# One tile per direction for the decay rows of a state-space mixer, summed and multiplied in place

## The chip, the cores and the metric

The kernel runs on one core of a Trainium2 chip. Its time is device microseconds (us) of one execution. A core has five engines with a queue of instructions each, worked off in order: TensorE (PE in the profile; PEld are its weight loads), VectorE (DVE), ScalarE (ACT), GpSimd (POOL) and SyncE (SP), which here issues most of the DMAs. They work on SBUF, a memory of 128 partitions; PE writes into PSUM. An engine that needs another's result waits at that instruction, and all behind it in its queue waits too.

## The reference, cut to what matters

The whole program is two layers of an encoder over 512 tokens with 1024 features: a mixer, a SwiGLU channel mixer and a gated embedding in each, then a norm. The change is in the first mixer, a Mamba-2 scan that runs over 8 groups of 4 heads, forwards and backwards. Within a chunk of 128 tokens one direction computes:

```python
acum = jnp.cumsum(dtc * a_gk, axis=1)
decay = jnp.exp(jnp.where(mask, acum[:, :, None] - acum[:, None], -jnp.inf))
cb = jnp.einsum('blgn,bsgn->blsg', cc, bc)
scores = cb[..., None] * decay * dtc[:, None]
y = jnp.einsum('blsgk,bsgkp->blgkp', scores, xc)
y = y + jnp.einsum('blgn,bgkpn->blgkp', cc, state) * jnp.exp(acum)[..., None]
```

So each head has a 128 by 128 matrix of decays per chunk and direction, masked to one triangle. `cb` belongs to the group and is the same for both directions but for the side of the mask. The kernel therefore adds the two decay matrices of a head first and multiplies the sum once by `cb`.

## The kernel before, in words

Features lie on the partitions and tokens along them, and the whole input stays in SBUF. Every fp32 product of a projection is made of three matmuls on a high and a low part of each factor (L292 to L294 and L677 to L679). The weights come in blocks of eight 128 by 128 tiles, 512 KB each: SP loads a block (L270), ACT casts the high part (L274), and DVE, or POOL for every other block of this mixer, subtracts it for the low part (L275). There are three buffers each for a raw block and its two parts, and a block is asked for two blocks before PE needs it.

The Python order of the program is the order in which work is given to a scheduler (the Tile framework's), which sets each engine's own order from dependences and its own estimate of when things are ready, and which gives out the buffers of the tiles. A tile waits for a buffer of its kind (its tag) until the readers of the buffer's last tile are done.

The mixer's loop runs over the groups g. In iteration g stand, in this order: the decay matrices of the group before (`mix_exp(g-1)`); the projections of group g with their convolution of five taps (`mix_in`, L591 on ACT, L595 on DVE, then the gate function at L597 and L598); the parts that come from the carried states (`mix_off`, L782 to L787); the projection of the output gate z (`mix_z`, L677 to L682); the diagonal products of the group before on its decay matrices (`mix_diag(g-1)`, L773 on PE, L775 on DVE, which adds the result into y); transposes and the matrix CB of group g (`mix_pre_a`, L688 to L707); at every odd g from 3 on the transposes of finished output (`finish`, L813 on PE into a PSUM buffer of the kind aux, of which there are four, then a cast at L323 on ACT and a subtraction at L324 on DVE); the output gate of the group before (`mix_gate`, L793 to L798: y times z, a tanh on ACT, the product, four sums of squares into `junk`); the first projections of the next group; and the chunk states (`mix_pre_b`, L723, copied out of PSUM into ST by ACT at L732 and L734 and carried on by POOL at L728 and DVE at L729, and y begun by POOL at L744).

`mix_exp` works on one head at a time. SP loads a tile FB of the head's two rows of 512 numbers, one per direction, repeated on every partition, 512 KB in all (L753). POOL sets the masked half of each direction to a value whose exponential is zero (L755, one instruction per direction), ACT takes the exponential per chunk with another bias each (L759, eight per head), DVE adds the two directions into a tile M (L761) and multiplies it by CB (L762). M stays until the diagonal products (L773). FB has 4 buffers of 4 KB per partition, M 4 of 2 KB. The same tags also serve the temporaries of the step sizes at the mixer's start (`dtt`, from L608) and, for FB, the split inputs `pp` of the gated embedding (L537); the second layer's embedding calls the same helper with its own tags (L912).

Of the kernel before, what the change touches and what calls it, by code (L numbers as in the profile page):

```python
# [10 lines left out]
F32 = mybir.dt.float32  # L11
F32R = mybir.dt.float32r
AF = mybir.ActivationFunctionType
ALU = mybir.AluOpType

P = 128
T = 512
# [6 lines left out]
NC = 4  # L24
# [191 lines left out]
def body(ctx, tc, d, out_):  # L216
    nc = tc.nc
# [314 lines left out]
    def ple_in(pool, i, tags):  # L532
        pr = {}
        for k in range(2):
            raw = pool.tile([P, T], F32, tag=tags[0], name="ppr", bufs=tags[3])
            (nc.scalar if i else nc.sync).dma_start(raw, d["pT"][i, k])
            pp = pool.tile([P, 2, T], F32R, tag=tags[1][k], name="pp", bufs=tags[2])  # L537
            pr[k] = split(raw, pp[:, 0], pp[:, 1])
        return pr
# [10 lines left out]
    def ssd(next_norm):  # L550
        pool = sctx.enter_context(tc.tile_pool(name="ssd", bufs=1))
        tags = ("pre", ("FB", "FB"), 4, 2)
# [55 lines left out]
        u = pool.tile([P, NC, 64], F32, tag="M", name="dtt", bufs=4)  # L608
        V.tensor_add(u, ps[:, 0:256].rearrange("p (c x) -> p c x", c=NC), pc("dtb", 0, 64).unsqueeze(1).broadcast_to([P, NC, 64]))

        na = pool.tile([P, NC, 64], F32, tag="M", name="dtt", bufs=4)
        V.scalar_tensor_tensor(na, u, -1.0, u, ALU.mult, ALU.min)
        e = pool.tile([P, NC, 64], F32, tag="M", name="dtt", bufs=4)
# [7 lines left out]
        q = pool.tile([P, NC, 64], F32, tag="M", name="dtt", bufs=4)  # L621
# [125 lines left out]
        def mix_exp(g, t):  # L747

            M = t["M"] = []
            for j in range(4):  # L750
                hd = 4 * g + j
                FB = pool.tile([P, 2, T], F32, tag="FB", name="FB", bufs=4)
                nc.sync.dma_start(FB, FRd[:, hd].partition_broadcast(P))  # L753
                for dr in range(2):
                    G.affine_select(FB[:, dr], FB[:, dr], pattern=[[0, NC], [1 - 2 * dr, P]], compare_op=ALU.is_ge,  # L755
                                    fill=BIG, base=0, channel_multiplier=2 * dr - 1)
                    for c in range(NC):
                        e = FB[:, dr, c * P:c * P + P]
                        A.activation(e, e, AF.Exp, bias=bcol[:, c, dr * 32 + hd:dr * 32 + hd + 1])  # L759
                m = pool.tile([P, T], F32, tag="M", name="M", bufs=4)  # L760
                V.tensor_add(m, FB[:, 0], FB[:, 1])  # L761
                V.tensor_mul(m, m, t["CB"].rearrange("p c x -> p (c x)"))  # L762
                M.append(m)
# [135 lines left out]
    def ple(i, nm, next_norm, prep):  # L899
        with tc.tile_pool(name=f"ple{i}", bufs=2) as pool:  # L900
# [11 lines left out]
            tags = ("pr", ("pp", "pp"), 2, 2)  # L912
# [245 lines left out]
```

## Time and profile before

| | |
|---|---|
| median of three runs | 1590.43 us |
| lowest and highest run | 1588.3 and 1595.03 us |
| the profiled execution, its whole time | 1591.31 us |
| the profiled execution, its span | 1589.5 us |
| PE busy | 1556.0 us, 98% of the span |
| DVE busy | 1064.6 us, 67% |
| ACT busy | 671.7 us, 42% |
| POOL busy | 195.0 us, 12% |

The span goes from the first to the last instruction of the profiled execution. The rest of its time lies around the span. The profile counts an engine as busy while an instruction of it runs, and lists the idle time in front of an instruction with what ended it. PE has a clock that the chip grants in stretches; the profile gives its mean as a part of the full 2.4 GHz, and 0.50 means 1.2 GHz. Most of PE's time is outside the first mixer, which runs from about 30 to 434 us. The engines take turns at setting PE's end there, so the stage is read by who waits for whom and not by the busy shares.

### The profile page before, as it was taken

Reading aid. Unit: us, or ns where it says so; the run is one execution under the profiler, and the core shown is the slowest. Engines: PE = TensorE matmul, PEld = TensorE weight load, DVE = VectorE, ACT = ScalarE, POOL = GpSimd, SP = SyncE. Lnnn points to the kernel's source line nnn. Section 1 sums busy time; section 2 is a strip of 40 time slices with the busy share of each in tenths; the row PEclk is TensorE's granted clock in tenths of the full one; section 3 lists DMA queues with packets and bytes.
Section 4 is the critical chain, followed back from the end, with each engine's and each line's share of the span. In section 5 each row is a group of like instructions: output and inputs, shape, how many; then the busy total and the mean of one; then the engine's idle time right before and its main releaser. Section 6 shows DMA issues by size and latency. Waiting matters only on the chain.

```text
span 1589.5 us, 19858 instructions
## 1 busy us (share of the span) xinstructions
PE 1556.0 (98%) x7698; PEld 1300.1 (82%) x7698; DVE 1064.6 (67%) x1463; ACT 671.7 (42%) x1111; POOL 195.0 (12%) x153
## 2 busy tenths in 40 slices
PE   7999999999999999999999999999999999999998
PEld 5888878888788788888888878788788888888887
DVE  6698997979845775564445678999864434434564
ACT  6486665647434322232233454343253223222355
POOL 1353444432100000000000002121000000000000
PEclk9999999999999999999999999999999999999999
DMA  7443343433233243243333344332223233233332
GB/s 244 121 145 110 119 132 106 115 104 100 86 116 113 85 138 122 94 153 103 96 93 98 110 159 144 106 107 93 67 90 96 93 95 105 93 95 103 113 101 79
DMA packets 56006, 176.53 MB, mean 111 GB/s; under 512 B 5959, under 2 KB 7175, under 8 KB 54760
## 3 DMA queue, kind: packets, MB, share of 16 engines
q1 hardware_dynamic: 46864, 151.17, 30.2%
q10 hardware_dynamic: 9048, 24.10, 4.3%
q8 instruction: 60, 0.98, 0.3%
q14 instruction: 34, 0.28, 0.1%
HBM read 164.63 MB, written 10.62 MB: 110 GB/s over the span
## 4 chain that ended last, share of the span: by engine, by line
PE 80%; DVE 10%; issue 3%; DMA 3%; ACT 2%; POOL 1%; ACTq 0%; POOLq 0%; DVEq 0%
PE mm_ps L292 23%; PE mm_ps L294 23%; PE mm_ps L293 23%; DMA FB<-FRd 2%; PE aux_ps L773 1%; PE mm_ps L678 1%; PE mm_ps L679 1%; PE mm_ps L677 1%; DVE pre L595 1%; PE aux_ps L782 1%; PE aux_ps L294 1%; PE aux_ps L293 1%; PE aux_ps L292 1%; DMA pjd<-ppo 1%; DVE w_lo L275 1%
## 5 line engine op out<-in xcount | busy, mean ns | idle before, releaser
L292 PE MATMUL mm_ps<-act,w_hi 128*128 128x512 f32 (+1 forms) x1856 | 724.9, 391 | 1.5 <-DVE hv L1022 1.0
L294 PE MATMUL mm_ps<-act,w_lo 128*128 128x512 f32 (+1 forms) x1856 | 717.2, 387 | 3.6 <-DVE w_lo L275 3.1
L293 PE MATMUL mm_ps<-act,w_hi 128*128 128x512 f32 (+1 forms) x1856 | 716.9, 386 | 0.9 <-DVE act L321 0.9
L274 ACT CAST w_hi<-w_raw 128x1024 fp32r<-128x1024 f32 x248 | 260.1, 1050 | 612.8 <-PE mm_ps L293 443.3
L292 PEld LDWEIGHTS mm_ps<-act,w_hi 128*128 128x128 f32 x1856 | 349.2, 188 | 77.7 <-issue 4.3
L294 PEld LDWEIGHTS mm_ps<-act,w_lo 128*128 128x128 f32 x1856 | 349.0, 188 | 75.7 <-DVE w_lo L275 4.0
L293 PEld LDWEIGHTS mm_ps<-act,w_hi 128*128 128x128 f32 x1856 | 349.1, 188 | 74.9 <-issue 3.6
L275 DVE TENSOR_TENSOR w_lo<-w_raw,w_hi 128x1024 fp32r<-128x1024 f32 x213 | 263.6, 1239 | 92.9 <-ACT w_hi L274 92.7
L275 POOL TENSOR_TENSOR w_lo<-w_raw,w_hi 128x1024 fp32r<-128x1024 f32 x35 | 86.4, 2468 | 781.0 <-ACT w_hi L274 781.0
L884 DVE TENSOR_TENSOR fb<-mm_ps,R 128x512 f32<-128x512 f32 x44 | 30.4, 691 | 128.8 <-PE mm_ps L294 128.8
L595 DVE SCALAR_TENSOR_TENSOR pre<-mm_ps,par,pre 128x511 f32<-128x511 f32 (+1 forms) x128 | 93.9, 741 | 6.7 <-ACT pre L591 5.9
L759 ACT ACTIVATE FB<-FB,bcol 128x128 f32<-128x128 f32 x256 | 79.8, 395 | 23.3 <-POOL FB L755 23.2
L881 DVE TENSOR_TENSOR fa<-mm_ps,R 128x512 f32<-128x512 f32 x44 | 30.3, 689 | 82.4 <-PE mm_ps L294 82.4
L892 DVE TENSOR_TENSOR h<-h,mm_ps 128x512 f32<-128x512 f32 x48 | 32.9, 686 | 72.4 <-PE mm_ps L294 72.4
L677 PE MATMUL mm_ps<-w_hi,act 128*128 128x256 f32 x256 | 73.7, 288 | 0.0
L678 PE MATMUL mm_ps<-w_lo,act 128*128 128x256 f32 x256 | 72.9, 285 | 0.5 <-DVE w_lo L275 0.5
L679 PE MATMUL mm_ps<-w_hi,act 128*128 128x256 f32 x256 | 72.4, 283 | 0.0
L755 POOL TENSOR_SCALAR_AFFINE_SELECT FB<-FB 128x512 f32<-128x512 f32 x64 | 53.3, 855 | 32.0 <-DMA FB<-FRd 23.7
L678 PEld LDWEIGHTS mm_ps<-w_lo,act 128*128 128x128 f32 x256 | 49.1, 192 | 1.0 <-DVE w_lo L275 0.7
L677 PEld LDWEIGHTS mm_ps<-w_hi,act 128*128 128x128 f32 x256 | 49.1, 192 | 0.2
L679 PEld LDWEIGHTS mm_ps<-w_hi,act 128*128 128x128 f32 x256 | 49.1, 192 | 0.0
L320 ACT CAST act<-fb 128x512 fp32r<-128x512 f32 x44 | 27.3, 622 | 32.0 <-DVE fb L885 32.0
(264 smaller groups left out, 1614.0 us busy)
## 6 DMA issues: line engine op xcount, KB each, us to landing
w_raw<-W SPq DMA_DIRECT2D x248, 512.0 KB, 3.5
FB<-FRd SPq DMA_DIRECT2D x32, 512.0 KB, 6.1
pjd<-ppo ACTq DMA_DIRECT2D x16, 256.0 KB, 2.7
Hd<-Ht ACTq DMA_DIRECT2D x4, 1024.0 KB, 4.1
Ht<-Hd ACTq DMA_DIRECT2D x4, 1024.0 KB, 4.8
pj<-pjd ACTq DMA_DIRECT2D x12, 256.0 KB, 3.6
h<-xT SPq DMA_DIRECT2D x8, 256.0 KB, 5.5
dec<-dec ACTq DMA_DIRECT2D x4, 512.0 KB, 3.8
```

What stands on the lines that cost most here:

```text
L274: A.copy(hi, raw)
L275: (G if pool_lo(b) else V).tensor_sub(lo, raw, hi.bitcast(F32))
L292: PE.matmul(ps, whi, xhi, start=start, stop=False)
L293: PE.matmul(ps, whi, xlo, start=False, stop=False)
L294: PE.matmul(ps, wlo, xhi, start=False, stop=stop)
L595: V.scalar_tensor_tensor(pre[:, a:b], ps[:, a + o:b + o], pc("cw", 5 * c + j), pre[:, a:b], ALU.mult, ALU.add)
L677: PE.matmul(o, xhi[:, cs], whi, start=k == 0 and c % 2 == 0, stop=False)
L678: PE.matmul(o, xhi[:, cs], wlo, start=False, stop=False)
L679: PE.matmul(o, xlo[:, cs], whi, start=False, stop=k == KD - 1 and c % 2 == 1)
L755: G.affine_select(FB[:, dr], FB[:, dr], pattern=[[0, NC], [1 - 2 * dr, P]], compare_op=ALU.is_ge, fill=BIG, base=0, channel_multiplier=2 * ...
L759: A.activation(e, e, AF.Exp, bias=bcol[:, c, dr * 32 + hd:dr * 32 + hd + 1])
L892: V.tensor_add(h[m], h[m], ps)
```

## The change

The tile FB of two directions becomes two tiles of one direction, 2 KB per partition each. Each is loaded by a DMA of its own (256 KB, still on SP) and goes through its select and its four exponentials alone. The sum of the two goes into the forward tile instead of into M, and the product with CB too; that tile is what the diagonal products read. M is gone. FB and M together took 4 x 4 + 4 x 2 = 24 KB per partition; the new FB has 12 buffers of 2 KB, 24 KB again. The temporaries `dtt` and the split inputs `pp` move to the new tag, `pp` as two tiles instead of one of twice the size; in the second layer two buffers of double size become four. The instructions on PE, DVE, ACT and POOL keep their number and shapes.

```diff
@@ ple_in
-            pp = pool.tile([P, 2, T], F32R, tag=tags[1][k], name="pp", bufs=tags[2])
-            pr[k] = split(raw, pp[:, 0], pp[:, 1])
+            pp = [pool.tile([P, T], F32R, tag=tags[1], name="pp", bufs=tags[2]) for _ in range(2)]
+            pr[k] = split(raw, *pp)
@@ ssd
-        tags = ("pre", ("FB", "FB"), 4, 2)
+        tags = ("pre", "FB", 12, 2)
...
-        u = pool.tile([P, NC, 64], F32, tag="M", name="dtt", bufs=4)
+        u = pool.tile([P, NC, 64], F32, tag="FB", name="dtt", bufs=12)
...
@@ mix_exp
-                FB = pool.tile([P, 2, T], F32, tag="FB", name="FB", bufs=4)
-                nc.sync.dma_start(FB, FRd[:, hd].partition_broadcast(P))
+                FB = []
                 for dr in range(2):
-                    G.affine_select(FB[:, dr], FB[:, dr], pattern=[[0, NC], [1 - 2 * dr, P]], compare_op=ALU.is_ge,
+                    f = pool.tile([P, T], F32, tag="FB", name="FB", bufs=12)
+                    nc.sync.dma_start(f, FRd[dr, hd:hd + 1].partition_broadcast(P))
+                    G.affine_select(f, f, pattern=[[0, NC], [1 - 2 * dr, P]], compare_op=ALU.is_ge,
                                     fill=BIG, base=0, channel_multiplier=2 * dr - 1)
                     for c in range(NC):
-                        e = FB[:, dr, c * P:c * P + P]
+                        e = f[:, c * P:c * P + P]
                         A.activation(e, e, AF.Exp, bias=bcol[:, c, dr * 32 + hd:dr * 32 + hd + 1])
-                m = pool.tile([P, T], F32, tag="M", name="M", bufs=4)
-                V.tensor_add(m, FB[:, 0], FB[:, 1])
+                    FB.append(f)
+                m = FB[0]
+                V.tensor_add(m, m, FB[1])
                 V.tensor_mul(m, m, t["CB"].rearrange("p c x -> p (c x)"))
@@ ple of the second layer
-            tags = ("pr", ("pp", "pp"), 2, 2)
+            tags = ("pr", "pp", 4, 2)
```

The scheduler puts the instructions of all engines but PE in another order in this mixer. PE's rows stay as they are up to the last group, and behind the mixer every engine's order is the same. The lines of `mix_exp` count on in the changed kernel: the load is L755, the select L756, the exponential L760, the sum L763 and the product L764, and what stood at L775 and behind stands two lines further down.

On ACT, at iteration 3, right behind the diagonal of the third group, from the copy of CB on (L323 is `finish`, L794 the tanh, L798 the squares, L591 the convolution's first step, L274 a weight cast), before:

```order
L702 COPY CB<-aux_ps 128x512
L323 ACTIVATE act<-aux_ps,par 128x512
L794 ACTIVATE z<-z 128x1024
L323 ACTIVATE act<-aux_ps,par 128x512
L759 ACTIVATE FB<-FB,bcol 128x128 x8
L798 ACTIVATE junk,ssq<-y 128x256 x4
L591 ACTIVATE pre<-mm_ps,par 128x512
L732 COPY ST<-aux_ps 128x256
L734 COPY ST<-aux_ps 128x256
L274 CAST w_hi<-w_raw 128x1024
```

and in the changed kernel, where the squares are L800 and the exponentials L760:

```order
L702 COPY CB<-aux_ps 128x512
L323 ACTIVATE act<-aux_ps,par 128x512
L760 ACTIVATE FB<-FB,bcol 128x128 x3
L323 ACTIVATE act<-aux_ps,par 128x512
L800 ACTIVATE junk,ssq<-y 128x256 x4
L760 ACTIVATE FB<-FB,bcol 128x128 x5
L274 CAST w_hi<-w_raw 128x1024
L591 ACTIVATE pre<-mm_ps,par 128x512
L732 COPY ST<-aux_ps 128x256
L734 COPY ST<-aux_ps 128x256
```

Eight exponentials stand between the casts of `finish` and the copies of ST in both; the squares now stand ahead of five of them, the tanh has moved further ahead, and a weight cast now stands in front of the copies.

On DVE, in the same place, from the weight subtraction ahead of the diagonal's results on (L775 takes these out of PSUM, L793 and L795 are the output gate, L707 weights the chunk inputs, L761 is the sum and L762 the product with CB), before:

```order
L275 TENSOR_TENSOR w_lo<-w_raw,w_hi 128x1024
L775 TENSOR_TENSOR y<-y,aux_ps 128x512
L761 TENSOR_TENSOR M<-FB 128x512
L775 TENSOR_TENSOR y<-y,aux_ps 128x512
L761 TENSOR_TENSOR M<-FB 128x512
L793 TENSOR_TENSOR y<-y,z 128x1024
L707 TENSOR_TENSOR xw<-XT,wS 128x3x256 x2
L324 SCALAR_TENSOR_TENSOR act<-aux_ps,par,act 128x512 x2
L795 SCALAR_TENSOR_TENSOR y<-z,y 128x1024
L762 TENSOR_TENSOR M<-M,CB 128x512 x2
L761 TENSOR_TENSOR M<-FB 128x512 x2
L762 TENSOR_TENSOR M<-M,CB 128x512
```

and in the changed kernel:

```order
L275 TENSOR_TENSOR w_lo<-w_raw,w_hi 128x1024
L777 TENSOR_TENSOR y<-y,aux_ps 128x512 x2
L795 TENSOR_TENSOR y<-y,z 128x1024
L707 TENSOR_TENSOR xw<-XT,wS 128x3x256 x2
L797 SCALAR_TENSOR_TENSOR y<-z,y 128x1024
L324 SCALAR_TENSOR_TENSOR act<-aux_ps,par,act 128x512 x2
L764 TENSOR_TENSOR FB<-FB,CB 128x512 x4
L763 TENSOR_TENSOR FB<-FB 128x512
L275 TENSOR_TENSOR w_lo<-w_raw,w_hi 128x1024
L595 SCALAR_TENSOR_TENSOR pre<-mm_ps,par,pre 128x510
```

The sums (L761 before) between the diagonal's results are gone from this place. The four products with CB stand in a row, and one sum (L763) stands ahead of a weight subtraction.

On POOL, in the first group (L744 begins y, L728 carries the states), before:

```order
L744 TENSOR_TENSOR y<-XT,par 128x1024
L275 TENSOR_TENSOR w_lo<-w_raw,w_hi 128x1024
L755 AFFINE_SELECT FB<-FB 128x512 x4
L728 TENSOR_TENSOR stt<-ST,eL 128x256 x2
L755 AFFINE_SELECT FB<-FB 128x512 x2
```

and in the changed kernel:

```order
L744 TENSOR_TENSOR y<-XT,par 128x1024
L756 AFFINE_SELECT FB<-FB 128x512 x2
L275 TENSOR_TENSOR w_lo<-w_raw,w_hi 128x1024
L756 AFFINE_SELECT FB<-FB 128x512 x4
L728 TENSOR_TENSOR stt<-ST,eL 128x256 x2
```

The two selects of the first head have moved ahead of a weight subtraction.

## Rows read from the trace of the kernel before

**Rows 1.** The page's first section: engine, busy us (share of span), instructions.

```profile
PE 1556.0 (98%) x7698; PEld 1300.1 (82%) x7698; DVE 1064.6 (67%) x1463; ACT 671.7 (42%) x1111; POOL 195.0 (12%) x153
```

**Rows 2.** Windows: us, PE PEld DVE ACT POOL busy (count), PEclk, DMA share, GB/s.

```profile
30.00:434.00 404.00, 394.72 (x2275) 336.63 (x2275) 349.95 (x499) 248.88 (x552) 148.75 (x126) 0.99 0.37 111
218.80:222.10 3.30, 3.19 (x12) 2.90 (x13) 3.16 (x8) 3.30 (x10) 1.76 (x3) 0.50 0.77 200
314.40:317.70 3.30, 3.30 (x10) 2.52 (x9) 3.30 (x7) 3.00 (x10) 1.36 (x3) 0.50 0.99 219
1101.90:1105.20 3.30, 3.26 (x28) 3.29 (x29) 3.30 (x5) 0.59 (x1) 0.00 (x0) 1.00 0.38 103
```

**Rows 3.** Timeline of PE: start, us, engine, line, operation, tiles, [idle before <-releaser].

```profile
92.79 0.50 PE L294 MATMUL mm_ps<-act,w_lo 128*128 128x512 f32 x1 [1.46 <-DVE w_lo L275]
...
218.91 0.90 PE L813 MATMUL aux_ps<-ident,y 128*128 128x128 f32 x3 [3.55 <-ACT ST L732]
...
313.31 0.44 PE L813 MATMUL aux_ps<-ident,y 128*128 128x128 f32 x2 [2.13 <-ACT ST L732]
...
1101.94 0.63 PE L1053 MATMUL aux_ps<-ident,act 128*128 128x128 f32 x4 [1.84 <-DVE act L1034]
```

**Rows 4.** Waits, 60 to 440 us: who <- for whom: us in total, times, longest.

```profile
POOL FB L755 <- DMA FB<-FRd: 23.7, 15, 5.8
ACT FB L759 <- POOL FB L755: 23.2, 12, 5.0
```

**Rows 5.** Waits of PE, 30 to 440 us.

```profile
PE aux_ps L813 <- ACT ST L732: 5.7, 2, 3.5
...
PE aux_ps L813 <- DVE act L324: 0.6, 1, 0.6
PE mm_ps L678 <- DVE w_lo L275: 0.5, 1, 0.5
```

**Rows 6.** Timeline of ACT, 204 to 220 us.

```profile
209.53 0.67 ACT L323 ACTIVATE act<-aux_ps,par 128x512 fp32r<-128x512 f32 x1
213.50 1.28 ACT L759 ACTIVATE FB<-FB,bcol 128x128 f32<-128x128 f32 x4 [3.30 <-POOL FB L755]
...
216.25 0.40 ACT L798 ACTIVATE junk<-y 128x256 f32<-128x256 f32 x1
...
218.51 0.35 ACT L732 COPY ST<-aux_ps 128x256 f32<-128x256 f32 x1
```

**Rows 7.** Chain of work that ended last, 0 to 480 us: start, us, what.

```profile
204.64 8.07 DMA FB<-FRd
...
300.45 6.35 DMA FB<-FRd
```

**Rows 8.** Tile FB, 0 to 440 us: count, ns min/median/max, first and last start.

```profile
L753 SPq DMA_DIRECT2D FB<-FRd x32: 359/377/1366, 68.8 to 362.2; - x32
L761 DVE TENSOR_TENSOR M<-FB x32: 676/690/2659, 85.2 to 407.3; 128x512 f32<-128x512 f32 x32
...
DMA to landing us min/median/max: 4.9/6.1/11.1
```

**Rows 9.** Waits of SP's DMA queue, 0 to 480 us.

```profile
SPq L270 <- DVE w_lo L275: 199.6, 39, 22.0
```

**Rows 10.** The page's DMA issues: count, KB each, median us to landing.

```profile
pjd<-ppo ACTq DMA_DIRECT2D x16, 256.0 KB, 2.7
```

**Rows 11.** Timelines of POOL and of ACT in the first group.

```profile
74.70 3.06 POOL L275 TENSOR_TENSOR w_lo<-w_raw,w_hi 128x1024 fp32r<-128x1024 f32 x1
...
89.49 1.04 ACT L274 CAST w_hi<-w_raw 128x1024 fp32r<-128x1024 f32 x1
```

**Rows 12.** Timelines of POOL and of DVE from 204 us.

```profile
204.14 2.70 POOL L275 TENSOR_TENSOR w_lo<-w_raw,w_hi 128x1024 fp32r<-128x1024 f32 x1 [6.57 <-ACT w_hi L274]
...
205.12 2.27 DVE L761 TENSOR_TENSOR M<-FB 128x512 f32<-128x512 f32 x1
...
213.21 1.33 DVE L795 SCALAR_TENSOR_TENSOR y<-z,y 128x1024 f32<-128x1024 f32 x1
```

More of the change, by code (lines that the diff above doesn't have):

```diff
@@ L606, in sm @@
             return pool.tile([P, NC, 64], F32, tag=name, name=name)
-        u = pool.tile([P, NC, 64], F32, tag="M", name="dtt", bufs=4)
+        u = pool.tile([P, NC, 64], F32, tag="FB", name="dtt", bufs=12)
         V.tensor_add(u, ps[:, 0:256].rearrange("p (c x) -> p c x", c=NC), pc("dtb", 0, 64).unsqueeze(1).broadcast_to([P, NC, 64]))
-        na = pool.tile([P, NC, 64], F32, tag="M", name="dtt", bufs=4)
+        na = pool.tile([P, NC, 64], F32, tag="FB", name="dtt", bufs=12)
         V.scalar_tensor_tensor(na, u, -1.0, u, ALU.mult, ALU.min)
-        e = pool.tile([P, NC, 64], F32, tag="M", name="dtt", bufs=4)
+        e = pool.tile([P, NC, 64], F32, tag="FB", name="dtt", bufs=12)
         elast = A.activation(e, na, AF.Exp)
@@ L620, in ssd @@
         V.tensor_mul(s2, s, s)
-        q = pool.tile([P, NC, 64], F32, tag="M", name="dtt", bufs=4)
+        q = pool.tile([P, NC, 64], F32, tag="FB", name="dtt", bufs=12)
         V.tensor_scalar_mul(q, s2, 1.0 / 19.0)
```

## The prediction

> **What bounds the kernel now.** I read the page's head first: TensorE (PE) is busy for 1556.0 us of a span of 1589.5 [rows 1], so only 33.5 us of the whole run are PE idle time, and a change that leaves PE's instructions alone can win no more than its share of them. The change touches the first mixer. The view by windows gives that stage, 30 to 434 us: PE 394.72 of 404.00 busy, so 9.28 us of idle time [rows 2]. The timeline of PE shows where most of it lies: 1.46 us before 92.79, 3.55 before 218.91, 2.13 before 313.31 [rows 3]; the other 2.1 us are six gaps of under 0.6. After the two long ones the granted clock is 0.50, that is 1.2 instead of 2.4 GHz, over windows of 3.3 us [rows 2]; half rate over 3.3 us loses 1.65 us each time, and this stands in the busy time, not in the idle time. So all that this stage can give back is 9.3 + 3.3 = 12.6 us, 0.8% of the run.
>
> Next, who causes the waits. In the list of waits GpSimd (POOL) waits 23.7 us for the FB loads and ScalarE (ACT) 23.2 us for POOL's selects on FB [rows 4], and PE 5.7 us, in two waits, for ACT's ST copies (L732) [rows 5]. The timeline of ACT around the longest one shows how these hang together: the cast at 209.53 is done at 210.20, then ACT stands 3.30 us before the exponentials at 213.50 [rows 6], since the FB load issued at 204.64 took 8.07 us [rows 7]; behind the exponentials queue the squares, the conv's first step and the ST copies at 218.51 [rows 6], and these free the PSUM buffer that PE's transposes (L813) want at 218.91. At 313.31 it is the same chain with a load of 6.35 us [rows 7]. Why is that load so late? It needs an FB buffer, which only the add into M frees, and the add needs an M buffer, which only the preceding group's diagonal products free. So every burst of loads starts just behind a diagonal, where ACT and DVE have most to do.
>
> **The change part by part.** *Buffers.* FB's 4 x 4 KB and M's 4 x 2 KB per partition become 12 x 2 KB: the same 24 KB. The add is in place, so it waits for no M; it frees the backward half at once, and the forward half stays as the masked matrix until its group's diagonal. Before, a group's adds all stand behind the diagonal of the group just ahead; in the new order, from the fourth group on, three of four stand ahead even of the diagonal before that one. This is the gain: work moves out of the burst.
>
> *Arithmetic.* The same 256 exponentials, 64 selects, 32 adds and 32 products, on the same shapes. PE's order is the same row by row up to the last group. Cost of this part: nothing on any engine.
>
> *Loads.* 32 loads of 512 KB become 64 of 256 KB: 32 more issues of 0.38 us [rows 8], 12.2 us on SP over 350 us. SP waits 199.6 us of the first 480 for weight subtractions alone [rows 9], which hides it; without that cover each issue would delay the weight load behind it by 0.38 us. What a half takes to land no row shows. Bounds: 2.7 us, another 256 KB transfer that overlaps little [rows 10], and 8.07, the load that hurt [rows 7]; the fastest whole load took 4.9 [rows 8]. I take 4.7: half the bytes, but a weight load or a second half beside it. The Trainium skill speaks against small loads (DMA: Bandwidth & Descriptors, Bandwidth: batch to 1 MiB or more; Anatomy of one DMA: about 2.0 us fixed plus bytes over 436 GB/s). By its figures a whole load would be an estimated 3.2 us and each half 2.6; the trace's 4.9 is above that, so the trace decides, and with the page's 2.6 the sum below would gain 1 us more.
>
> *First group.* POOL starts the weight subtraction at 74.70 and it lasts 3.06 us [rows 11]; in the new order two selects of the first head stand ahead of it, not behind. The first load was issued at 68.84 and a whole one takes at least 4.9 [rows 8], so its halves are there by 74.7: ACT's first exponentials start near 75.4 instead of 78.4. Then the subtraction comes in between, and the other three heads start near 79.6: 24 exponentials of 0.31 (four in 1.28 us [rows 6]) and a tanh of 0.6 end near 87.7, where ACT's weight cast stands at 89.49 now [rows 11]. DVE's subtraction of that block comes 1.7 us earlier with it, and PE's 1.46 us there [rows 3], with 0.28 just before, shrink to about 0.2. Gain 1.5 us; between 0 (the first half late) and 1.74.
>
> *The wait at 218.91.* PE could go on at 218.91 - 3.55 = 215.4. The loads that ACT meets here will wait for PE's diagonal alone and no longer for a DVE add behind it: the first goes out near 203.9 instead of 204.64. With 4.7 us it lands at 208.6; POOL, free from 206.84 [rows 12], selects until 209.2; three exponentials and the second cast (0.67) end near 211. The squares also need y from DVE, done at 214.5 now [rows 12]: two adds ahead of it are gone, but the y*z product now meets POOL's subtraction that ends at 206.84, the one that stretched an add to 2.27 us [rows 12]. I put y at 211.5. Then squares and conv step 2.2 us (216.3 to 218.5 now [rows 6]), five exponentials 1.6, one weight cast of 1.0 that the new order puts ahead of the copies, and a copy of 0.35: 216.7. PE waits 1.4 instead of 3.55: gain 2.1. At 2.7 us per half the wait would be 0.9; at 8.07 the chain ends near 219.5, and PE waits 4.1, 0.6 longer than now. *The wait at 313.31* by the same steps: PE ready at 311.2, copy done near 312.6, wait 1.4 instead of 2.13, gain 0.7; between a gain of 1.2 and a loss of 0.6. *The clock.* The two drops followed idle times of 3.55 and 2.13 us; 1.84 us before 1101.94 was followed by full clock, 1.00 [rows 2, 3]. Waits of 1.4 us should leave it: gain 2 x 1.65 = 3.3, or 0.
>
> *Small gaps.* Waits of 0.5 and 0.6 us lie behind DVE work that the burst crowds [rows 5], and near the last group's end no add is left. Of the 2.1 us I take 0.7.
>
> *Against it.* The adds now stand amid the conv steps; DVE takes its queue in order, so an exponential that is late holds the conv steps, the PSUM evictions and the weight subtractions behind the add, and PE after them. And the last half of each group is released only by a diagonal. I book 1 us for it, with ends at 0 and 12 (below).
>
> Sum: 1.5 + 2.1 + 0.7 + 3.3 + 0.7 - 1.0 = 7.3 us less. The profiled execution took 1591.3 us, of which 1589.5 are the span; the median of the runs is 1590.43, 0.9 lower. I set the sum against the median: 1583.1, and say **1583 us**.
>
> **The rivals.** *All waits go* (chance 0.15): the halves land in under 4 us and ACT never meets one that is missing; 1590.4 - 12.6 = 1577.8. For it: most of the exponentials leave the burst. Against: ACT has as many instructions as now between the diagonal and the copies, plus one cast.
>
> *The wait stays* (0.25): the change does not do what it says, since the last half of a group still needs a diagonal, as M did, and lands 8 us later, behind a weight load and beside three other halves. Then the first group's 1.5 us and perhaps 0.5 of small gaps are won, and 0.6 is lost twice: 1590.4 - 0.8 = 1589.6. For it: the 8.07 stood beside weight loads, and the new order has them too.
>
> *Slower* (0.10): the add of a group's last head stands directly ahead of a weight subtraction on DVE. It is ready at landing + 0.64 + four exponentials, the last of them behind the squares; DVE gets there about 13 us after the diagonal. If landing passes 8 us, towards the 11.1 of the slowest load here [rows 8], DVE idles up to 3 us at each of six groups. DVE is idle for 404.00 - 349.95 = 54 us of the stage [rows 2], so part of it is caught up; I count 2 us each as reaching PE: 12 less 1.5 of the first group, 1601. A second thing pulls the same way: the 64 selects spread over stretches in which DVE adds and multiplies, and an add, 0.69 in the median, took 2.27 beside a POOL operation [rows 8, 12]. The Trainium skill (SBUF — State Buffer, SBUF: two separate sides) calls the port pair of the two engines an exclusive lock, held for a whole instruction; the trace agrees, as that add ended 0.55 after POOL's 206.84. By the rule a meeting costs up to one POOL instruction, and a select of 0.64 is too short to decide alone.
>
> **How the numbers follow.** Forecast 0.50 (own range 1580 to 1586), all waits go 0.15, the wait stays 0.25, slower 0.10. A measurement of this kernel can tell about 0.5%, 8 us, from no change: faster means below 1582.5. That takes the 0.15 and about half of the forecast's 0.50: 0.39. The other half and the rival that keeps the wait give 0.51 for the same, and 0.10 is slower. The range leaves out the slower case and the very ends: 1578 to 1591.
>
> **What would show it.** Right: PE's gap at the first group under 0.5 us; the two long gaps under 1.9 us with granted clock 1.00 behind them; ACT's wait before the exponentials that follow the cast of the odd groups under 1 us; POOL's wait for FB well under 23.7 us; FB landing in the median between 3.5 and 5 us. Wrong: an FB landing of 6 us or more in spite of half the size, a PE wait for ACT's ST copies of over 3 us, or DVE idle time before the adds (L763) that PE repeats a few us later.

## The result, and the profile after

The changed kernel took **1600.86 us** (median of four runs, 1600.54 to 1601.71) against 1589.37 for the kernel before on the same chip: a ratio of 1.007, with a 95% interval of 1.0056 to 1.0084. Forecast were 1583 us with a range of 1578 to 1591. The change makes the kernel slower by 0.7%, and the time is outside the range. It is the number of the rival named "slower" (1601), but by luck: that rival needed halves that land after 8 us or more, and the slowest half that the profile shows took 5.5. The losses that the experiments show lie elsewhere.

The page's head after, to be read beside [rows 1]:

```profile
PE 1562.9 (98%) x7698; PEld 1304.8 (82%) x7698; DVE 1068.1 (67%) x1463; ACT 670.5 (42%) x1111; POOL 210.0 (13%) x153
```

The span is 1599.2 us, 9.7 longer (the medians of the runs lie 11.5 apart). PE does the same 7698 matmuls, yet it is busy 6.9 us longer: the clock, as the windows below show. Only 2.8 us more are idle time. POOL has the same 153 instructions and is busy 15 us longer, so some of them last longer.

The timeline of PE after, at the waits that matter (start, us, engine, line, operation, tiles, count, idle before with its releaser), beside [rows 3]:

```profile
94.63 0.51 PE L294 MATMUL mm_ps<-act,w_lo 128*128 128x512 f32 x1 [3.62 <-DVE w_lo L275]
172.97 0.48 PE L723 MATMUL aux_ps<-xw,BT 128*128 128x256 f32 x1 [1.63 <-DVE xw L707]
175.63 0.77 PE L723 MATMUL aux_ps<-xw,BT 128*128 128x256 f32 x1 [1.96 <-DVE xw L707]
227.46 0.66 PE L815 MATMUL aux_ps<-ident,y 128*128 128x128 f32 x4 [1.72 <-ACT ST L732]
310.99 0.69 PE L695 MATMUL aux_ps<-ident,sx 128*128 128x128 f32 x2 [2.56 <-DVE y L777]
323.39 0.66 PE L815 MATMUL aux_ps<-ident,y 128*128 128x128 f32 x4 [0.55 <-ACT ST L732]
...
439.16 0.39 PE L294 MATMUL mm_ps<-act,w_lo 128*128 128x512 f32 x1
```

The fourth and the sixth of these are the two long waits of [rows 3], for the ST copies: 3.55 became 1.72, and 2.13 became 0.55. This is what the change was forecast to do. The first is the first group's wait, which was to vanish and grew to 3.62. The others are new. The last row stands just behind the mixer, and before the same matmul stood here:

```profile
431.69 0.39 PE L294 MATMUL mm_ps<-act,w_lo 128*128 128x512 f32 x1
```

So the mixer ends 7.5 us later. The other 2.2 us of the 9.7 come behind it, where all orders are the same; 1.5 of them arise at a stretch of half clock near 1136 us, which a second trace of the changed kernel does not have (`after_again`, below).

Busy time by windows after (us, then PE, PEld, DVE, ACT and POOL busy with counts, granted clock, DMA share, GB/s):

```profile
95.50:98.80 3.30, 3.30 (x9) 2.60 (x8) 3.30 (x5) 0.39 (x2) 2.69 (x2) 0.50 0.78 191
174.00:180.70 6.70, 5.07 (x8) 2.77 (x9) 6.70 (x7) 4.38 (x16) 5.62 (x5) 0.50 0.34 134
224.00:228.00 4.00, 2.28 (x10) 0.97 (x9) 4.00 (x6) 4.00 (x12) 2.68 (x4) 1.00 0.00 0
310.50:313.80 3.30, 2.81 (x13) 2.81 (x14) 3.27 (x3) 2.05 (x4) 2.37 (x1) 0.50 0.74 209
323.00:327.00 4.00, 3.61 (x20) 3.17 (x21) 4.00 (x7) 3.53 (x12) 2.45 (x2) 1.00 0.36 87
1010.30:1013.50 3.20, 3.20 (x9) 2.49 (x8) 3.20 (x7) 2.98 (x5) 0.00 (x0) 0.50 0.98 347
```

The clock stays at full rate behind the two waits for ST, as forecast. But at each of the three places where waits grew or are new there is a stretch at 1.2 GHz, and three more that the kernel before does not have lie outside the mixer: near 1010 (the last row), 17 and 1136 us. At half rate a stretch loses half of its busy time: 1.65, 2.5 and 1.4 us in the mixer.

From the starts of PE the 7.5 us of the mixer add up roughly: 3.5 in the first group (94.63 less 92.79, and the clock behind it), 7 near 173 (waits of 0.9 shortly before, 1.63 and 1.96, and the clock), 4 near 311, less 3.5 and 3.2 at the two waits for ST (1.8 and 1.6 of idle time, 1.65 of clock each) and some 0.5 of small gaps.

### The profile page after: what moved, and what is told of

It reads as the page before. It is cut to its first block, busy times and chain, and to the rows that moved or that the text cites. A ratio compares the mean times of both kernels' runs of the same rounds, so it can differ in the third digit from the quotient of the medians.

```text
span 1599.2 us, 19907 instructions
## 1 busy us (share of the span) xinstructions
PE 1562.9 (98%) x7698; PEld 1304.8 (82%) x7698; DVE 1068.1 (67%) x1463; ACT 670.5 (42%) x1111; POOL 210.0 (13%) x153
## 4 chain that ended last, share of the span: by engine, by line
PE 80%; DVE 10%; issue 4%; ACT 3%; DMA 2%; POOL 1%; SPq 0%; ACTq 0%; POOLq 0%; DVEq 0%
PE mm_ps L292 23%; PE mm_ps L294 23%; PE mm_ps L293 23%; DMA FB<-FRd 1%; PE aux_ps L775 1%; DVE xw L707 1%; PE mm_ps L678 1%; PE mm_ps L677 1%; PE mm_ps L679 1%; PE aux_ps L294 1%; PE aux_ps L293 1%; PE aux_ps L292 1%; PE aux_ps L784 1%; DVE w_lo L275 1%; DVE act L321 1%
## 5 line engine op out<-in xcount | busy, mean ns | idle before, releaser
L274 ACT CAST w_hi<-w_raw 128x1024 fp32r<-128x1024 f32 x248 | 260.1, 1050 | 610.8 <-PE mm_ps L293 445.1
L275 POOL TENSOR_TENSOR w_lo<-w_raw,w_hi 128x1024 fp32r<-128x1024 f32 x35 | 93.7, 2676 | 739.2 <-ACT w_hi L274 739.2
L760 ACT ACTIVATE FB<-FB,bcol 128x128 f32<-128x128 f32 x256 | 81.0, 392 | 58.6 <-POOL FB L756 58.6
L756 POOL TENSOR_SCALAR_AFFINE_SELECT FB<-FB 128x512 f32<-128x512 f32 x64 | 58.3, 929 | 71.1 <-DMA FB<-FRd 53.9
```

What stands on the lines that cost most here:

```text
L274: A.copy(hi, raw)
L275: (G if pool_lo(b) else V).tensor_sub(lo, raw, hi.bitcast(F32))
L756: G.affine_select(f, f, pattern=[[0, NC], [1 - 2 * dr, P]], compare_op=ALU.is_ge, fill=BIG, base=0, channel_multiplier=2 * dr - 1)
```

## Three chains behind the new waits

**Near 173 us.** The timelines of DVE, SP, POOL, ACT, DVE again and POOL again, in this order, follow one half tile of FB:

```profile
160.85 0.69 DVE L763 TENSOR_TENSOR FB<-FB 128x512 f32<-128x512 f32 x1 [0.26 <-ACT FB L760]
...
161.57 0.32 SPq L755 DMA_DIRECT2D FB<-FRd  x1
...
164.91 1.50 POOL L756 TENSOR_SCALAR_AFFINE_SELECT FB<-FB 128x512 f32<-128x512 f32 x1 [5.47 <-DMA FB<-FRd]
...
166.45 1.28 ACT L760 ACTIVATE FB<-FB,bcol 128x128 f32<-128x128 f32 x4 [4.24 <-POOL FB L756]
167.64 1.06 ACT L682 ACTIVATE z<-mm_ps 128x512 f32<-128x512 f32 x2
...
170.01 1.09 ACT L696 COPY XT<-aux_ps 128x512 f32<-128x512 f32 x2
...
171.12 4.36 DVE L707 TENSOR_TENSOR xw<-XT,wS 128x768 f32<-128x768 f32 x2 [5.21 <-ACT XT L696]
...
169.72 2.39 POOL L275 TENSOR_TENSOR w_lo<-w_raw,w_hi 128x1024 fp32r<-128x1024 f32 x1 [3.30 <-ACT w_hi L274]
172.06 2.61 POOL L744 TENSOR_TENSOR y<-XT,par 128x1024 f32<-128x1024 f32 x1
```

A sum ends at 161.5 and frees a half tile; the load goes out at 161.57 and lands 3.2 us later; POOL, which waited 5.47 us, masks it; ACT, which waited 4.24 us, takes its four exponentials at 166.45; only then come the copies of z and XT, which were ready before, then xw on DVE, and PE had to wait. The load at 161.57 is the 31st of 64: it belongs to the fourth group's last head. The group whose XT is being copied here is the third, and the fourth group's diagonal is two diagonals away. So ACT stood still for work that nobody needed for some 90 us.

The late load is not all of it. The two xw take 4.36 us together, while POOL subtracts weights and begins y beside them (the last two rows). In the kernel before no work of POOL ran beside them, and they took:

```profile
164.68 1.81 DVE L707 TENSOR_TENSOR xw<-XT,wS 128x768 f32<-128x768 f32 x2
```

PE's second wait here, 1.96 us before 175.63, is for the second xw. That POOL slows them is argued from the first group (below), not shown by a run of its own. A slow xw alone does not make PE wait: without the late load (`a_noload35`, below) the two take 3.95 us, start at 165.94, and PE has no wait at L723.

**Near 311 us** it is the same, one step longer (timelines of DVE, SP, POOL, ACT, DVE). The load is the 55th, of the seventh group:

```profile
300.93 0.68 DVE L763 TENSOR_TENSOR FB<-FB 128x512 f32<-128x512 f32 x1
...
301.63 0.32 SPq L755 DMA_DIRECT2D FB<-FRd  x1
...
305.68 0.64 POOL L756 TENSOR_SCALAR_AFFINE_SELECT FB<-FB 128x512 f32<-128x512 f32 x1 [5.95 <-DMA FB<-FRd]
...
306.35 1.28 ACT L760 ACTIVATE FB<-FB,bcol 128x128 f32<-128x128 f32 x4 [4.28 <-POOL FB L756]
...
310.26 1.28 DVE L777 TENSOR_TENSOR y<-y,aux_ps 128x512 f32<-128x512 f32 x2
```

Behind the exponentials wait the convolution's gate, a weight cast, and with them on DVE the last gate product, a weight subtraction and the reading of the diagonal out of PSUM; PE's next transposes (L695) need that PSUM buffer.

**In the first group** it is another thing. The timelines of DVE and POOL after:

```profile
85.44 1.80 DVE L763 TENSOR_TENSOR FB<-FB 128x512 f32<-128x512 f32 x2
87.16 1.11 DVE L764 TENSOR_TENSOR FB<-FB,CB 128x512 f32<-128x512 f32 x1
...
93.36 1.22 DVE L275 TENSOR_TENSOR w_lo<-w_raw,w_hi 128x1024 fp32r<-128x1024 f32 x1
...
85.00 3.76 POOL L756 TENSOR_SCALAR_AFFINE_SELECT FB<-FB 128x512 f32<-128x512 f32 x4
```

and the same two places before:

```profile
85.16 0.68 DVE L761 TENSOR_TENSOR M<-FB 128x512 f32<-128x512 f32 x1
...
91.08 1.65 DVE L275 TENSOR_TENSOR w_lo<-w_raw,w_hi 128x1024 fp32r<-128x1024 f32 x1
...
90.61 1.04 POOL L755 TENSOR_SCALAR_AFFINE_SELECT FB<-FB 128x512 f32<-128x512 f32 x1 [5.82 <-DMA FB<-FRd]
```

The sums and products start at the same time, but the weight subtraction behind them, for which PE waits, starts 2.3 us later. Before, POOL's next selects began at 90.61, when DVE was nearly done. Now the second group's halves are there early, POOL masks four of them from 85.00 on, and both engines take longer: a product 1.11 us, a select 0.94.

How far the exponentials run ahead is seen in the view of the tile FB, cut off at about 200 us, shortly before the third group's diagonal: it counts those that had started by then (line, engine, operation, count: duration in ns min/median/max, first and last start). The kernel before:

```profile
L759 ACT ACTIVATE FB<-FB,bcol x128: 385/393/414, 78.4 to 191.2; 128x128 f32<-128x128 f32 x128
```

The changed kernel:

```profile
L760 ACT ACTIVATE FB<-FB,bcol x152: 384/389/413, 76.3 to 200.2; 128x128 f32<-128x128 f32 x152
```

The changed kernel with the edge of `a_holdCB` (below):

```profile
L760 ACT ACTIVATE FB<-FB,bcol x96: 386/397/410, 76.2 to 180.8; 128x128 f32<-128x128 f32 x96
```

The kernel before with the edges of `b_mix` (below):

```profile
L761 ACT ACTIVATE FB<-FB,bcol x96: 384/391/409, 79.2 to 175.9; 128x128 f32<-128x128 f32 x96
```

A group has 32. Only three groups, 96, are needed by then. The kernel before was one group ahead; the changed one is nearly two.

## The experiments

All times are medians beside runs of the kernel before on the same chip (1588.4 to 1589.8 us); the ratio is to these. The theories: **A**, the order, in which exponentials stand ahead of urgent work on ACT and wait there for loads; **B**, collisions of POOL and DVE; **C**, the 64 small loads by themselves.

**Exponentials held behind their own group's CB copy** (`a_holdCB`). Tiles and loads are those of the changed kernel; an edge in the scheduler puts the exponentials behind an instruction on ACT:

```diff
-            A.copy(CB, ps)
+            t["hold"] = A.copy(CB, ps)
...
-                        A.activation(e, e, AF.Exp, bias=...)
+                        after(t["hold"], lambda: A.activation(e, e, AF.Exp, bias=...))
```

> The changed kernel, with one edge added: on ScalarE the exponentials of a group may not stand ahead of that group's own copy of CB (L702). Tiles, loads, selects and sums stay. Theory A (order): the changed kernel lost its time because exponentials of a later group stood on ScalarE ahead of the copies of z and XT and of the conv's gate, and waited there for a half tile whose load a sum had released late. Then TensorE's waits before L723 (3.6 us near 173) and before L695 (2.6 us near 311) go, and the half clock behind them: 6 to 10 us back, 1591 to 1595; the wait of 3.6 us in the first group stays, and the two waits for the ST copies may come back in part, since the exponentials now pile up between CB and ST. Theory B (collisions): the selects, now spread out, slow VectorE everywhere; then the order matters little and it stays at 1598 to 1603. Theory C (loads): 64 small loads cost the time by themselves; also 1598 to 1603.

Measured: **1584.35 us**, ratio 0.9964 (0.9949 to 0.9978). That is 16 us less than without the edge, below the kernel before and below A's range (1591 to 1595). All waits of PE from 60 to 441 us by the list of waits (who <- for whom: us, times, longest):

```profile
PE mm_ps L294 <- DVE w_lo L275: 3.6, 1, 3.6
PE aux_ps L784 <- DVE ST L729: 0.5, 1, 0.5
PE aux_ps L638 <- issue: 0.2, 1, 0.2
```

The new waits are gone, and the two for ST did not come back, though A had thought they might in part. C falls: the loads are as many and as small. Collisions (B) are left for the 3.6 us of the first group; elsewhere none makes PE wait here.

**Held behind the last ST copy** (`a_holdST`): the edge starts at L734 instead of L702.

> The changed kernel, with one edge added: on ScalarE the exponentials of a group may not stand ahead of that group's last ST copy (L734). Theory A (order): no exponential of a later group stands ahead of urgent copies any more, neither those of z and XT nor those of ST, so the waits near 173, 227 and 311 all go under 1 us and no half clock is left between 130 and 440 us: 1585 to 1591; only the first group's 3.6 us stay. Theory B (collisions) and theory C (loads): 1597 to 1603, since selects and loads are as many and as spread.

Measured: 1587.96 us, ratio 0.9989 (0.9979 to 0.9999), as A said. The waits near 173, 227 and 311 are gone, and the first group's are down to 1.7 and 0.3 us, for its weight casts now stand ahead of the exponentials; but 1.55 us are new at three places (183, 275 and 368 us), where PE waits for a weight cast behind the crowd of exponentials. So ST is too late a place, except for the first group.

**Half tiles, but the sum into M** (`a_halfM`):

```diff
...
-                    f = pool.tile([P, T], F32, tag="FB", name="FB", bufs=12)
+                    f = pool.tile([P, T], F32, tag="FB", name="FB", bufs=8)
...
-                m = FB[0]
-                V.tensor_add(m, m, FB[1])
+                m = pool.tile([P, T], F32, tag="M", name="M", bufs=4)
+                V.tensor_add(m, FB[0], FB[1])
```

> The changed kernel's half tiles and 64 loads of 256 KB, but the sum goes into a tile M of its own as in the kernel before (8 half tiles and 4 M, the same 24 KB). A sum again needs the M of the group ahead, which its diagonal products free. Theory A (order, brought about by the sum in place): no exponential can run a period ahead, so TensorE's waits near 173 and 311 are not there; the two waits for the ST copies are as before (3.5 and 2.1 us) or a little shorter, and the time is that of the kernel before within 4 us: 1585 to 1593. Theory C (loads): the small loads cost the time, 1597 to 1603. Theory B (collisions): in between, about 1594.

Measured: 1594.85 us, ratio 1.0031 (1.002 to 1.0041), 2 us above A's range, below C's, and just the number of B. By the time alone it would be B; the trace speaks for A. In it the waits near 173 and the one before L695 are absent, as A said, those for ST are 2.4 us each, the first group's is 2.1, PE waits 1.0 us for another DVE step near 309, and PE leaves the mixer within 0.1 us of the kernel before. But the profiled execution, 1592.29, is one of the three fastest of twelve (1591.2 to 1596.93). Those three had a mean granted clock of 0.996, the other nine 0.993 to 0.995, so more half clock goes with at least part of their longer time; where it fell no trace shows.

**Sum in place, but whole tiles and loads** (`b_pair`): the kernel before with 6 tiles FB of 4 KB, no M.

```diff
...
-                FB = pool.tile([P, 2, T], F32, tag="FB", name="FB", bufs=4)
+                FB = pool.tile([P, 2, T], F32, tag="FB", name="FB", bufs=6)
...
-                m = pool.tile([P, T], F32, tag="M", name="M", bufs=4)
-                V.tensor_add(m, FB[:, 0], FB[:, 1])
+                m = FB[:, 0]
+                V.tensor_add(m, m, FB[:, 1])
```

> The kernel before with the sum and the product in place, but tiles and loads of both directions kept whole (512 KB each, 6 buffers of 4 KB, no M). The backward half stays held until the diagonal products, so only two heads of the next group can run ahead. Theory A (order): two heads ahead means fewer exponentials ahead of urgent copies than in the changed kernel, but those that are there wait longer (6 us per load): 1590 to 1598. Theory C (loads): without the small loads the time is that of the kernel before, 1587 to 1592. Theory B (collisions): 1590 to 1594.

Measured: 1596.52 us, ratio 1.0039 (1.0024 to 1.0054): in A's range, but not for A's reason. Its largest waits of PE from 30 to 441 us:

```profile
PE mm_ps L294 <- DVE w_lo L275: 4.7, 1, 4.7
PE aux_ps L813 <- ACT ST L732: 4.3, 2, 2.1
PE aux_ps L723 <- ACT ST L732: 2.1, 1, 2.1
```

Without small loads the first group's wait is there all the same, even larger. POOL's selects of the second group run beside DVE here too, from 85.48 on; DVE's weight subtraction starts at 92.75 and takes 3.37 us, with POOL's own weight subtraction beside it from 92.41. So the sum in place lets the second group's selects come early, whatever the size of the loads; whether they cause the wait asked for an experiment of its own.

**Without the second group's selects** (`a_nosel1`):

```diff
-                    G.affine_select(f, f, ...
+                    g == 1 or G.affine_select(f, f, ...
...
-                        A.activation(e, e, AF.Exp, bias=bcol[...])
+                        A.activation(e, e, AF.Exp, bias=eps_t if g == 1 else bcol[...], scale=0.0 if g == 1 else 1.0)
```

> The changed kernel without the eight masking selects of the second group on GpSimd (its exponentials read a constant in their place, so that group's decays are not computed; the order of TensorE, ScalarE, VectorE and SyncE is the same row by row). This is for the first group's wait, 3.62 us before 94.63, where the kernel before had 1.46 and 0.28. Theory B1 (collision): GpSimd's selects run from 85.0 to 88.8 and at 89.4 beside the sums and products of VectorE and stretch them from 0.69 to 1.11 us each; without them VectorE ends its eight instructions near 91.3 instead of 93.4, the wait falls to 1.5 to 1.9 us and no half clock follows: 2 to 4 us off the total, 1596.5 to 1599. Theory B2 (late start): VectorE is late because the exponentials or the sums start late; then the wait stays above 3 us and the time at 1599.5 to 1602.

Measured: 1597.38 us, ratio 1.0043 (1.0031 to 1.0056), 3.5 us below the changed kernel, within B1. DVE and PE in the first group (timelines):

```profile
85.31 1.28 DVE L763 TENSOR_TENSOR FB<-FB 128x512 f32<-128x512 f32 x2
86.51 0.68 DVE L764 TENSOR_TENSOR FB<-FB,CB 128x512 f32<-128x512 f32 x1
...
90.98 1.22 DVE L275 TENSOR_TENSOR w_lo<-w_raw,w_hi 128x1024 fp32r<-128x1024 f32 x1
...
92.25 0.50 PE L294 MATMUL mm_ps<-act,w_lo 128*128 128x512 f32 x1 [1.36 <-DVE w_lo L275]
```

The start is the same (85.31 against 85.44), each sum and product is back at 0.68 or 0.69, the subtraction starts at 90.98 instead of 93.36, and PE waits 1.36 us instead of 3.62. Behind the first group PE is 4.0 us ahead of the changed kernel. With the orders of PE, ACT, DVE and SP unchanged this shows the collision as the cause. The Trainium skill (SBUF — State Buffer, SBUF: two separate sides) calls the port pair an exclusive lock that is held for a whole instruction; the trace agrees in kind: the product beside selects takes 1.11 instead of 0.68, and each select there 0.94, where the median of all 64 before was 0.64. Neither loses a whole instruction of the other: 0.43 and 0.30 us.

**Without loads and selects of the fourth and sixth group** (`a_noload35`):

```diff
-                    nc.sync.dma_start(f, FRd[dr, ...
-                    G.affine_select(f, f, ...
+                    g in (3, 5) or nc.sync.dma_start(f, FRd[dr, ...
+                    g in (3, 5) or G.affine_select(f, f, ...
...
-                        A.activation(e, e, AF.Exp, bias=bcol[...])
+                        A.activation(e, ident, AF.Exp, bias=eps_t, scale=0.0) if g in (3, 5) else A.activation(e, e, AF.Exp, bias=bcol[...])
```

> The changed kernel in which the half tiles of the fourth and the sixth group are neither loaded nor masked (their exponentials read a constant, so these decays are not computed); the exponentials keep their number and nearly their places on ScalarE, ahead of the copies of z and XT. Theory A1 (the stuck load): what held ScalarE near 166 and 306 was the load of a half that had waited for a sum; without loads the exponentials there run at once, TensorE's waits before L723 (3.6 us) and L695 (2.6) go, and the half clock behind them: 6 to 11 us off, 1590 to 1595, with the first group's 3.6 us still there. Theory A2 (the place alone): four exponentials of 0.31 us ahead of urgent copies are too many wherever they stand; then half of these waits stays and the time is 1596 to 1600.

Measured: 1590.47 us, ratio 1.0004 (0.9995 to 1.0013), 10 us below the changed kernel, as A1 said. The timeline of ACT and that of PE, at the places of the first chain:

```profile
159.90 0.69 ACT L760 ACTIVATE FB<-ident,eps_t 128x128 f32<-128x128 f32 x2
160.50 1.06 ACT L682 ACTIVATE z<-mm_ps 128x512 f32<-128x512 f32 x2
...
170.62 0.81 PE L723 MATMUL aux_ps<-xw,BT 128*128 128x256 f32 x3
```

Exponentials still stand ahead of z, but run at once, and PE has no wait at L723. That settles that the stuck load is what brought the wait near 173. For the one near 311 this run was misaimed: the load that ends late there is the seventh group's, not the sixth's as I had assumed. That load is still waited for, 4.06 us on ACT, though the wait at L695 is gone too, since ACT comes to it earlier. For this one only the runs with edges speak.

**Both edges** (`a_mix`): behind CB, and for the first group behind its last ST copy.

> The changed kernel with the exponentials of a group held back on ScalarE behind that group's copy of CB, and those of the first group behind its last ST copy. With the first edge alone it took 1584.35 us, and its only long waits in the mixer were the first group's 3.58 us with half clock behind it, about 4 us in all; with the exponentials behind the ST copy the first group waited 1.7 and 0.3 us. Theory A: both add up, no half clock between 80 and 440 us, 1580 to 1583. If instead the first group's wait only moves (to the weight blocks behind it), it stays at 1583 to 1586.

Measured: **1581.56 us**, ratio 0.9942 (0.9928 to 0.9955). In the mixer PE waits 1.1 us at one place and at most 0.5 at others, and there is no half clock in it: at the mixer's end PE is 12.2 us ahead of the kernel before, nearly all of the 12.6 that the prediction named. The whole run gains less, 8.2 us by the medians; in the trace 2.6 us are lost again behind the mixer, half of them at a half clock near 1117 us. Both edges add up.

**The kernel before, held behind ST** (`b_holdST`), and **with both edges** (`b_mix`): the same edits in the kernel before, with whole tiles and M.

> The kernel before (whole tiles, M, 32 loads) with one edge: on ScalarE the exponentials of a group not ahead of that group's last ST copy. Theory A says that ScalarE's order is what matters and the tiles matter little: the two waits for the ST copies (3.55 and 2.13 us) and the half clock behind them go, 5 to 9 us off, 1581 to 1585, unless the exponentials then come too late for the diagonal products. The rival, that the halves and the sum in place are what made room: then the exponentials, 32 of them behind the ST copies with loads of 6 us, are late for the diagonal or hold back the weight casts, and it is 1588 to 1595.

> The kernel before (whole tiles, M) with the two edges that made the changed kernel fast: exponentials behind the group's copy of CB, those of the first group behind its last ST copy. Theory A: the kernel before already runs its exponentials behind CB, since its loads start at a diagonal, so the first edge does nothing there: the waits of 3.55 and 2.13 us for the ST copies stay with their half clock, only the first group gains its 1.5 to 2.5 us; 1586 to 1589. Then the tiles of the change are worth 5 to 7 us as soon as the order is held (the changed kernel with these edges took 1581.56). The rival, that the edges alone do it and the tiles are worth nothing: 1580 to 1583.

Measured: 1586.8 us, ratio 0.9977 (0.9968 to 0.9986), and **1580.02 us**, ratio 0.9951 (0.9935 to 0.9966). The first lies between theory A and its rival, with the same waits for weight casts as `a_holdST`, 1.1 us each. The second was a miss: I expected 1586 to 1589, since I thought that the kernel before had its exponentials behind their own CB already. It had them behind the CB of the group before theirs (128 done, above). Held to their own group they no longer meet a late load, and all waits of PE of over 0.2 us from 60 to 441 us are:

```profile
PE mm_ps L678 <- DVE w_lo L275: 1.2, 1, 1.2
PE mm_ps L678 <- POOL w_lo L275: 0.6, 1, 0.6
PE aux_ps L784 <- DVE ST L729: 0.5, 1, 0.5
```

With whole loads and M, the waits for ST are gone too. Beside each other, 0.9942 and 0.9951 with intervals that overlap: once the order is held to the own group, the tiles of the change are worth nothing that can be measured.

**One group ahead** (`a_holdprev`): the changed kernel, with the edge at the CB copy of the group before.

> The changed kernel with an edge that lets the exponentials run one group ahead, as in the kernel before, but not further: those of a group not ahead of the CB copy of the group before it on ScalarE. Held to their own group they took 1584.35 us, unheld 1600.9. Theory A (how far ahead): none may stand ahead of the copies of z and XT of the group before, so TensorE's waits before L723 and L695 go with their half clock (10 us), while exponentials of the next group still stand between CB and the ST copies, as in the kernel before, and the waits for ST (1.7 and 0.6 us unheld) stay or grow to 2 us; the first group's 3.6 us stay: 1589 to 1594. The rival (it is only luck where the order falls): no relation to the distance, anything between 1584 and 1601.

Measured: 1584.37 us, ratio 0.9968 (0.9957 to 0.9978), the same as with the group's own CB, and below what A expected. 128 exponentials are done at the third diagonal, as in the kernel before; but the waits for ST did not come back. ACT waits for selects once, 2.7 us, against 23.2 in [rows 4]. So at the same distance of one group the changed tiles do what they were to do: their loads are early enough. It is the second group of distance that costs. What the tiles alone are worth at one group is not shown, since no run puts this edge into the kernel before.

**The changed kernel again** (`after_again`).

> The changed kernel once more, on the chip of this call, for its spread and for a second trace. Theory A: the waits of TensorE stand at the same places with the same sizes within 0.3 us (first group 3.6, before L723 1.6 and 2.0, before L695 2.6), since the orders of the engines are fixed; 1598 to 1603. What may differ are stretches of half clock outside the mixer (near 17, 1010 and 1136 us), which the first trace shows and the kernel before does not: if they are there again they belong to the change, if not they fell so by chance.

Measured: 1601.19 us (1598.07 to 1603.44), ratio 1.0078 (1.006 to 1.0096). The waits in the mixer are the same within 0.3 us (3.62, 1.60, 1.96, 2.44), though the half clock at the first group lasts twice as long. Outside the mixer half clock came again near 1012 us, where both traces of the changed kernel have a wait of 1.87 and 1.88 us and [rows 3]'s trace has one of 1.65 without; near 17 and 1136 it did not come again, so these fell by chance (more on the clock in the last section). Why the wait at 1010 is longer in these two traces stays open; the orders there are the same.

## Why the prediction was wrong, step by step

*The bound* held: 12.6 us to be won in the mixer, and `a_mix` wins 12.2 of them.

*The waits for ST and the clock behind them* were right. Forecast were 1.4 and 1.4 us of wait and 6.1 us of gain; 1.72 and 0.55 came, the clock stayed at 1.00, and some 6.7 us were won. FB's halves land in 4.1 us in the median, 4.7 were taken; the other estimate given there, 2.6 us, lies below the fastest half (3.0). Two things were luck. The 0.55 owes something to the loss ahead of it, where the half clock near 311 held PE back: in `a_nosel1`, with the same orders on PE, ACT and DVE but no half clock there, the second wait for ST is 1.71 us. And that waits of 1.4 us leave the clock alone held for the ST copies, but not for every wait (last section).

*First group* failed in sign: 1.5 us of gain forecast, some 3.5 of loss measured. The step looked at ACT and at POOL's subtraction, and at where DVE's subtraction comes; it did not ask what POOL would do beside DVE once buffers come free earlier. The mechanism stood in the text, as "a second thing" of the slower rival, priced as too short to decide. `a_nosel1` shows that it decides there: nine short instructions in a row lose 2.3 us, and the stretch at half clock behind the longer wait costs 1.65 more.

*Against it* is the term that failed most: 1 us was booked, some 11 came (7 near 173, 4 near 311). The text had read from the new order that three of four sums stand "ahead even of the diagonal before that one", and booked this as the gain alone. It rightly saw that sums in the convolution would let a late exponential hold things up, but placed the damage on DVE, in front of a weight subtraction at each group. It fell on ACT, which takes its queue in order too: exponentials that nobody needed yet stood ahead of copies that PE waited for. The change made room for this: in place, a sum frees a half tile at once, so the scheduler drew the exponentials nearly two groups forward, and each then depended on a sum a few us ahead, a load of 3 to 4 us and a select. For the wait near 311 this rests on the chain in the trace and the runs with edges. POOL's wait for FB, which was to fall well below 23.7 us, rose, and so did ACT's for the selects:

```profile
ACT FB L760 <- POOL FB L756: 58.6, 22, 4.7
POOL FB L756 <- DMA FB<-FRd: 53.9, 18, 6.5
```

*The cause of the old waits* was read too narrowly: late loads, for want of M. `b_mix` removes the waits with M and whole loads in place. The load was late only for exponentials that were a group early; the profile could have told it, by the count of exponentials done when a diagonal starts.

*The chances:* slower got 0.10. It had the sums that hold up other work and the collisions, but its price of 1601 fits by luck: it was made of 2 us at each of six groups less a gain in the first group, while the mixer lost 3.5, 7 and 4 us at three places and won 6.7 at two. The rival by which the change does not do what it says was wrong: it does, and it does more than that.

## What to carry to other kernels

Buffers that come free earlier are also a permission to run ahead, and an engine that works its queue in order pays for early work whenever that work has to wait for a load. When a change loosens a buffer, count how far ahead the early work then stands, and look at what is queued behind it. An edge that holds it to its own iteration can be worth more than the buffers: here two such edges took 0.5% off the kernel before and 1.2% off the changed one (1581.56 against 1600.86).

## What the runs showed of the hardware

A product of 128 x 512 on DVE took 1.11 us instead of 0.68 while POOL masked tiles of the same size, and the selects took 0.94 instead of 0.64, so that both lose.

The length of a wait alone did not tell whether PE fell to 1.2 GHz. In the mixer, over all thirteen traces, single waits of up to 1.73 us never came with half clock and the seven of 3.55 us or more always did; of the ten between 2.07 and 2.56 six did. The wait before L695 near 311, 2.56 us in the changed kernel, came with it (310.50 to 313.80, above), but 2.46 us at the same place in `a_nosel1` did not:

```profile
306.50:309.80 3.30, 3.30 (x25) 2.95 (x26) 3.27 (x2) 1.34 (x3) 2.32 (x1) 1.00 0.76 260
```

Waits of 1.63 and 1.96 us in a row came with 6.7 us at half clock. Behind the mixer every trace has a wait of 1.31 us between 1115 and 1136 us, and nine of the thirteen have half clock behind it; a wait of 1.8 to 1.9 us some 25 us ahead of it came with none in any. So a microsecond or two between two runs can be the clock alone.
